# Loading operands ahead at four seams of a split-precision MLP

## The chip, the cores and the metric

The kernel runs on one core of a Trainium2 chip. The metric is the device time of one execution in microseconds (us), as the median of several runs. A core has five engines that run side by side and wait for each other only through semaphores: TensorE (PE in the profile) does matrix products, VectorE (DVE) elementwise work, ScalarE (ACT) copies and activations, GpSimd (POOL) here issues the stores and does some elementwise work, and SyncE (SP) issues the loads. Each engine takes its instructions in the order in which the program put them. The transfers of all queues run on 16 DMA engines.

## The reference

The reference is one layer of an encoder over 2304 tokens (256 and 2048) of width 1024: two mixers, an output projection, and a squared-ReLU MLP with a hidden width of 4096.

```python
def trunk(x, norm1_g, w_in, ...):
    h = rmsnorm(x, norm1_g[l])
    proj = h @ w_in[l]
    ...
    y = jnp.concatenate([ya, yb], axis=-1).astype(x.dtype) @ w_out[l]
    x = x + y
    h = rmsnorm(x, norm2_g[l])
    x = x + jnp.square(jax.nn.relu(h @ w_ff1[l])) @ w_ff2[l]
    return rmsnorm(x, norm_f_g)
```

Everything is fp32. The change touches the last three lines and the way into them.

## The kernel before

**How a product is made.** TensorE works on a rounded 32-bit type (`F32R`). An fp32 operand x is split in two: a high part, which ACT makes by a copy (the instruction `act` on line 83), and a low part, which DVE makes as x minus the high part (`tt`, line 68). `split` does both. `mm3` (lines 176, 179 and 180) adds three products: high by high, high by low, low by high.

**The MLP** is two products of block matrices, each made by a scheme with seven half-sized products in place of eight. In the first product (hidden = h @ w_ff1) the tokens go in three *thirds* (2, then 1, then 0), 2 x 384 tokens each, and a third has 16 *units* of hidden columns; the loop counter n runs from 0 to 47. A unit is seven products p, in the order 1, 6, 2, 7, 5, 3, 4, and each product is 12 matmuls of 128x384. So a unit is 84 matmuls.

- The operands on the token side, one pair of tiles `oh` and `ol` for each p, stay for a whole third. `prep` normalises the tokens (`x1_d`), transposes them and stores their sums as `h2_d` (in the profile h_d); `load_hop` loads them from there in two halves of 128x768 into `xg` tiles and splits each half. There are four `xg` buffers, so SP can have four such loads ahead of the splits.
- The weights come as `w1r` (straight) and `w1t` (sums, stored in `t1_d`), loaded a unit ahead, and each product's weights are split into a tile `w` just before it (six buffers).
- Behind each product, DVE adds it to the others (`u`, `c`), ACT squares it (`hid`), DVE makes the sums (`his`), and POOL stores both in `s2_d` (in the profile s_d).
- `w2_terms` prepares sums of w_ff2 for the second product, once in every second unit from n = 16 on, through `xg` and `gt` tiles.

**The second product** takes its operands two units (one q) at a time: `operands` loads a 128x1280 piece of `s2_d` into a `gt` tile (three buffers) and a 128x1024 piece of weights into an `xg` tile, and splits them into `sh`, `sl`, `th`, `tl`. One q is 30 matmuls of 128x512 over five token blocks j. The residual is loaded from `x1_d` (ten tiles `x1` of 512 KB; x in the profile's names) and added at the end.

**What sets the order.** The program is written as a list of operations; a scheduler decides by a simulated timeline in which order each engine gets them, and tile pools decide which buffer an operation has to wait for. Pools are opened and closed like a stack, so a pool that is opened after another was closed can lie where the other was, and its first writers wait for the last readers of the old tiles. `order(a, b)` and `hold` add an order by hand.

**The seams** that the change touches: (A) the end of the output projection (`out_proj`, `xr` tiles) to the first unit, where lines 1211 to 1217 load and split the seven operands of third 2; (B) third 2 to third 1, and the same from third 1 to third 0, where `load_hop(third - 1, p)` (line 1266) follows the last use of operand p; (C) the first product to the second, where the pools close (line 1270) and the tiles of `operands` are new.

## Time and profile before

| | us |
|---|---|
| median of 3 runs (2749.1 to 2764.31) | 2754.13 |
| the profiled execution | 2757.29 |
| its span, first to last instruction | 2755.5 |
| PE busy | 2602.6 (94%) |
| DVE busy | 1966.1 (71%) |
| ACT busy | 1395.7 (51%) |
| POOL busy | 403.1 (15%) |

Times in the trace are microseconds from the start of the span. The first unit of the MLP begins at 1304.67; seam B lies near 1580, the next one between thirds near 1820, seam C near 2055. A row of a table by stretches gives the stretch and its length, then each engine's busy time and count of instructions, the clock granted to TensorE (1.00 is 2.4 GHz, 0.50 is 1.2 GHz), the busy share of the DMA engines and GB/s. In a row of the timeline an idle time in brackets names what ended it. "pm" and "px_..." are PSUM tiles, "tr", "f2" and "g2" their banks; matmuls overlap, so a mean of one is longer than the distance to the next.

### The profile page before, as it was taken

Reading aid. Unit: us, or ns where it says so; the run is one execution under the profiler, and the core shown is the slowest. Engines: PE = TensorE matmul, PEld = TensorE weight load, DVE = VectorE, ACT = ScalarE, POOL = GpSimd, SP = SyncE. Lnnn points to the kernel's source line nnn. Section 1 sums busy time; section 2 is a strip of 40 time slices with the busy share of each in tenths; the row PEclk is TensorE's granted clock in tenths of the full one; section 3 lists DMA queues with packets and bytes.
Section 4 is the critical chain, followed back from the end, with each engine's and each line's share of the span. In section 5 each row is a group of like instructions: output and inputs, shape, how many; then the busy total and the mean of one; then the engine's idle time right before and its main releaser. Section 6 shows DMA issues by size and latency. Waiting matters only on the chain.

```text
span 2755.5 us, 49048 instructions
## 1 busy us (share of the span) xinstructions
PE 2602.6 (94%) x17846; PEld 2346.1 (85%) x17846; DVE 1966.1 (71%) x5478; ACT 1395.7 (51%) x2608; POOL 403.1 (15%) x666
## 2 busy tenths in 40 slices
PE   6997999879999999999899999999999999999998
PEld 5885699759899987787899899999998888888887
DVE  4783599859899888466888887787765455555564
ACT  5553211248778776234776566666555334344342
POOL 1241223232111111222122011111110000000000
PEclk9999999999999999999899999999999999999999
DMA  9576754488546456799798798898788555775662
GB/s 253 181 240 204 233 175 147 154 235 245 177 149 227 167 193 227 258 336 345 263 321 304 256 343 303 289 348 319 292 309 283 175 172 171 244 239 190 196 224 75
DMA packets 352498, 651.81 MB, mean 237 GB/s; under 512 B 67264, under 2 KB 231744, under 8 KB 346112
## 3 DMA queue, kind: packets, MB, share of 16 engines
q1 hardware_dynamic: 282272, 355.34, 40.2%
q0 software_dynamic: 69984, 293.33, 29.5%
q8 instruction: 141, 2.31, 0.3%
q14 instruction: 101, 0.83, 0.1%
HBM read 428.68 MB, written 219.87 MB: 235 GB/s over the span
## 4 chain that ended last, share of the span: by engine, by line
PE 60%; issue 16%; DVE 8%; DMA 7%; ACT 4%; POOL 4%; SPq 1%; POOLq 0%; DVEq 0%; ACTq 0%
PE pm L176 8%; PE pm L180 8%; PE pm L179 8%; PE px_g L180 3%; PE px_g L176 3%; PE px_g L179 3%; PE px_fl L176 3%; PE px_fl L179 3%; PE px_fl L180 3%; PE px_f L179 3%; PE px_f L180 3%; PE px_f L176 3%; PE px_tr L179 2%; PE px_tr L180 2%; PE px_tr L176 2%
## 5 line engine op out<-in xcount | busy, mean ns | idle before, releaser
L68 DVE TENSOR_TENSOR sl<-gt,sh 128x1280 fp32r<-128x1280 f32 (+1 forms) x112 | 152.1, 1358 | 291.4 <-ACT sh L83 288.9
L83 ACT ACTIVATE sh<-gt 128x1280 fp32r<-128x1280 f32 (+1 forms) x112 | 130.8, 1168 | 393.5 <-PE pm L179 155.8
L176 PE MATMUL px_f<-oh,w 128*128 128x384 f32 x672 | 227.0, 339 | 5.1 <-ACT oh L83 5.1
L180 PE MATMUL pm<-oh,w 128*128 128x384 f32 x672 | 226.5, 337 | 4.3 <-DVE w L68 4.3
L179 PE MATMUL pm<-ol,w 128*128 128x384 f32 x672 | 226.7, 338 | 3.9 <-DVE ol L68 3.9
L176 PE MATMUL pm<-oh,w 128*128 128x384 f32 x672 | 226.3, 338 | 3.7 <-ACT oh L83 3.7
L180 PE MATMUL px_f<-oh,w 128*128 128x384 f32 x672 | 227.5, 339 | 0.8 <-DVE w L68 0.7
L179 PE MATMUL px_f<-ol,w 128*128 128x384 f32 x672 | 227.2, 339 | 0.5 <-DVE ol L68 0.5
L179 PE MATMUL pm<-hl,whi 128*128 128x384 f32 x576 | 201.0, 349 | 7.1 <-DVE hl L80 7.1
L176 PE MATMUL pm<-hh,whi 128*128 128x384 f32 x576 | 198.7, 350 | 7.4 <-ACT sg L83 3.8
L180 PE MATMUL pm<-hh,wlo 128*128 128x384 f32 x576 | 197.9, 345 | 0.0
L83 ACT ACTIVATE sel<-KQ 128x384 f32<-128x384 f32 (+1 forms) x312 | 168.4, 560 | 50.8 <-DVE KQ L68 48.9
L68 DVE TENSOR_TENSOR KQ<-KQ,Fl 128x384 f32<-128x384 f32 x288 | 154.5, 553 | 9.2 <-ACT sel L83 6.9
L83 ACT ACTIVATE w<-w1t 128x512 fp32r<-128x512 f32 x192 | 120.0, 628 | 79.7 <-PE pm L180 43.3
L83 ACT ACTIVATE c<-c 128x384 f32<-128x384 f32 x192 | 99.9, 523 | 100.3 <-DVE c L68 99.5
L176 PE MATMUL pm<-th,sh 128*128 128x512 f32 x384 | 149.7, 391 | 0.0
L68 DVE TENSOR_TENSOR st<-st,pr 128x32 f32<-128x32 f32 (+1 forms) x1016 | 149.6, 202 | 0.0
L179 PE MATMUL pm<-tl,sh 128*128 128x512 f32 x384 | 149.4, 389 | 0.0
L180 PE MATMUL pm<-th,sl 128*128 128x512 f32 x384 | 149.4, 389 | 0.0
L176 PE MATMUL px_g<-th,sh 128*128 128x512 f32 x368 | 143.2, 389 | 0.0
L179 PE MATMUL px_g<-tl,sh 128*128 128x512 f32 x368 | 143.2, 389 | 0.0
L180 PE MATMUL px_g<-th,sl 128*128 128x512 f32 x368 | 143.2, 389 | 0.0
(369 smaller groups left out, 7374.6 us busy)
## 6 DMA issues: line engine op xcount, KB each, us to landing
gt<-s_d SPq DMA_DIRECT2D x112, 384.0 KB
xg<-in_w_ff_dram SPq DMA_DIRECT2D x80, 512.0 KB
s_d<-his POOLq DMA_DIRECT2D x48, 768.0 KB, 7.8
w1t<-t_d SPq DMA_DIRECT2D x32, 1024.0 KB
xg<-t_d SPq DMA_DIRECT2D x64, 512.0 KB
hh<-h_hi POOLq DMA_DIRECT2D x42, 768.0 KB, 7.4
hl<-h_lo POOLq DMA_DIRECT2D x42, 768.0 KB, 6.5
s_d<-hid POOLq DMA_DIRECT2D x48, 576.0 KB, 4.5
```

The source lines that it names most:

```text
L68: ins = V.tensor_tensor(out=o, in0=a, in1=b, op=op)
L83: S.activation(out=o, in_=i, func=f, **kw)
L176: ins = T.matmul(o, ah, bh, start=first, stop=False)
L179: T.matmul(o, ah, bl, start=False, stop=False)
L180: return T.matmul(o, al, bh, start=False, stop=last)
```

## The change

In six parts:

1. The weight pool of the earlier stages, `wp`, is cut from six buffers to four, and two go to a pool `wpb` that is closed earlier (`swb.close()`), so that its room is free when the MLP's pools open.
2. The weights of the first two products of unit 0 are split before the projection's pools close (`first`), into two buffers of a pool that is already open; the six `w` buffers are now 2 + 4. Five of the seven token-side tiles lie in the early pool (four before), and are named by slot and not by p.
3. `load_hop` becomes `raw_hop` (the loads) and `split_hop`. The first half of an operand goes through an `xg` tile, the second half through a `gt` tile.
4. At the two seams between thirds the loads run three operands ahead of the splits.
5. `w2_terms` runs in other units (`W2N` in place of 16, 18, ... 46): none in the first or the last unit of a third (n = 16, 31, 32, 47).
6. The operands of the first two q of the second product are split into old tiles of the first product (the tiles of products 1 and 6, then 2 and 7), before the pools close. The ten residual loads wait for the last matmul of the second q.

The core of the diff:

```diff
-    wp = sww.enter_context(tc.tile_pool(name="wp", bufs=6, reuse_waits="tile"))
+    wp = sww.enter_context(tc.tile_pool(name="wp", bufs=4, reuse_waits="tile"))
+    swb = ExitStack()
+    wpb = swb.enter_context(tc.tile_pool(name="wpb", bufs=2, reuse_waits="tile"))
...
-    def load_hop(third, p):
-        pool = hsa if p in (1, 5, 6, 7) else hsb
-        hop[p] = [pool.tile([P, 4, TB], F32R, name=f"o{x}{p}", tag=f"o{x}{p}") for x in "hl"]
-        for k in range(0, 4, 2):
-            ld = xtile()[:, :2 * TB].rearrange("p (k t) -> p k t", k=2)
+    def slot(pool):
+        return [pool.tile([P, 4, TB], F32R, name=f"o{x}{len(slots)}", tag=f"o{x}{len(slots)}") for x in "hl"]
+
+    def raw_hop(third, p):
+
+        out = []
+        for i, k in enumerate(range(0, 4, 2)):
+            ld = (gtile(2 * TB) if i else xtile()[:, :2 * TB]).rearrange("p (k t) -> p k t", k=2)
             nc.sync.dma_start(out=ld, in_=h2_d[third][:, POS[p], k:k + 2])
-            split(ld, hop[p][0][:, k:k + 2], hop[p][1][:, k:k + 2])
+            out.append(ld)
+        return out
+
+    def split_hop(p, raw, tiles):
+        hop[p] = tiles
+        for i, ld in enumerate(raw):
+            split(ld, tiles[0][:, 2 * i:2 * i + 2], tiles[1][:, 2 * i:2 * i + 2])
...
-    W2S = 16
+
+    W2N = [17, 19, 21, 23, 24, 25, 27, 29, 33, 35, 37, 39, 40, 41, 43, 45]
     ORDER = (1, 6, 2, 7, 5, 3, 4)
+
+    def wtile(x):
+
+        w = (wr1 if x % 6 < 2 else wr).tile([P, 2, 4, P], F32R, name="w", tag="w", bufs=2 if x % 6 < 2 else 4)
+        return w[:, 0], w[:, 1]
...
-    for p in (1, 6, 7, 5):
-        load_hop(2, p)
+    for p in (1, 6, 2, 7, 5):
+        slots.append(slot(hsa))
+        split_hop(p, raw_hop(2, p), slots[-1])
     for b in (1, 0):
         out_proj(b, *out_prep(b, op), op, "f2")
     st6.close()
+    first = [split(w1[0][p], *wtile(x)) for x, p in enumerate(ORDER[:2])]
...
-                wh, wl = split(wt[p], w[:, 0], w[:, 1])
+                wh, wl = first.pop(0) if first else split(wt[p], *wtile(7 * (n - 1) + x))
...
                 if i == NP2 - 1 and third:
-                    load_hop(third - 1, p)
+
+                    if x == 0:
+                        ahead = [raw_hop(third - 1, q) for q in ORDER[:3]]
+                    split_hop(p, ahead.pop(0), hop[p])
+                    if x + 3 < len(ORDER):
+                        ahead.append(raw_hop(third - 1, ORDER[x + 3]))
...
+    early = []
+    for q, (a, b) in enumerate(((1, 6), (2, 7))):
+        (sh, sl), (th, tl) = hop[a], hop[b]
+        early.append(operands(1, q, 0, 5 * P, [t.rearrange("p k t -> p (k t)")[:, :n].rearrange("p (e c) -> p e c", e=2)
+                                               for t, n in ((sh, 1280), (sl, 1280), (th, 1024), (tl, 1024))]))
+    st8.close()
+    st7.close()
...
-        for j in js:
-            for n in range(2):
+        def residuals(after):
+            for j, n in [(j, n) for j in js for n in range(2)]:
                 xt[j, n] = x1p.tile([P, D], F32, name="x1", tag="x1")
-                nc.sync.dma_start(out=xt[j, n], in_=x1_d[tok[j][n]])
+                ld = nc.sync.dma_start(out=xt[j, n], in_=x1_d[tok[j][n]])
+                order(ld, after, mybir.DependencyClass.Sync)
...
             for q in range(late):
-                ops = operands(p, q, j0 * P, j1 * P)
+                ops = early.pop(0) if early else operands(p, q, j0 * P, j1 * P)
                 for j in js:
-                    products(q, j, ops)
+                    mm = products(q, j, ops)
+                if p == 1 and q == 1:
+                    residuals(mm)
```

Up to seam A the engines' orders are the same but for names. What moves at the seams is shown at three places.

DVE at seam A before, from the last additions of the output projection (`xr`) on; `ol1` and `ol6` are low parts of token-side operands of products 1 and 6, `w` low parts of weights, `w1t` sums of the next unit's weights:

```order
L68 TENSOR_TENSOR xr_17291<-xr_17291,px_f2_17307 128x512
L68 TENSOR_TENSOR ol1_17100<-xg_17101,oh1_17099 128x768
L68 TENSOR_TENSOR xr_17322<-xr_17322,px_f2_17324 128x512
L68 TENSOR_TENSOR xr_17322<-xr_17322,px_f2_17338 128x512
L68 TENSOR_TENSOR w1t_17400<-w1r_17399 128x512 x2
L68 TENSOR_TENSOR w_17414<-w1r_17091,w_17414 128x512
L68 TENSOR_TENSOR w_17431<-w1t_17092,w_17431 128x512
L68 TENSOR_TENSOR w1t_17400<-w1r_17399,w1t_17400 128x512
L68 TENSOR_TENSOR w_17448<-w1r_17091,w_17448 128x512
L68 TENSOR_TENSOR w_17468<-w1t_17092,w_17468 128x512
L68 TENSOR_TENSOR w_17485<-w1t_17092,w_17485 128x512
L68 TENSOR_TENSOR w_17506<-w1r_17091,w_17506 128x512
```

and in the changed kernel, where `ol0` to `ol4` belong to products 1, 6, 2, 7, 5:

```order
L68 TENSOR_TENSOR xr_17305<-xr_17305,px_f2_17321 128x512
L68 TENSOR_TENSOR ol0_17104<-xg_17105,oh0_17103 128x768
L68 TENSOR_TENSOR ol1_17114<-xg_17115,oh1_17113 128x768
L68 TENSOR_TENSOR ol2_17124<-xg_17125,oh2_17123 128x768
L68 TENSOR_TENSOR ol3_17134<-xg_17135,oh3_17133 128x768
L68 TENSOR_TENSOR w1t_17410<-w1r_17409 128x512 x2
L68 TENSOR_TENSOR w_17452<-w1r_17095,w_17452 128x512
L68 TENSOR_TENSOR xr_17336<-xr_17336,px_f2_17338 128x512
L68 TENSOR_TENSOR xr_17336<-xr_17336,px_f2_17352 128x512
L68 TENSOR_TENSOR w1t_17410<-w1r_17409,w1t_17410 128x512
L68 TENSOR_TENSOR w_17472<-w1t_17096,w_17472 128x512
L68 TENSOR_TENSOR w_17489<-w1t_17096,w_17489 128x512
```

Four first halves stand ahead of the projection's last two additions, where one stood, and the low parts of the first two products' weights are no longer in this place. Behind the piece shown there stand another `w`, a `w1t`, `ol4` and then the second halves, `ol0` from `gt_17107` first.

SP at seam B before, from the loads of unit 17's weights (`w1r_20486`, `w1t_20487`) on; the operands of products 1 and 6 were loaded earlier, `xg_20342` is the first half of product 2:

```order
L1186 DMA w1r_20486<-in_w_ff1_dram 128x4x256
L1163 DMA xg_20342<-h2_d1_261 128x768
L1163 DMA xg_20346<-h2_d1_261 128x768
L1187 DMA w1t_20487<-t1_d_266 128x2048
L1163 DMA xg_20369<-h2_d1_261 128x768
L1163 DMA xg_20373<-h2_d1_261 128x768
L1163 DMA xg_20400<-h2_d1_261 128x768
L1163 DMA xg_20404<-h2_d1_261 128x768
L1185 DMA w1r_20635<-in_w_ff1_dram 128x4x128
```

and now, where `xg_20328` is the first half of product 5 and `gt_20305` the second half of product 7:

```order
L1198 DMA w1r_20464<-in_w_ff1_dram 128x4x256
L1169 DMA xg_20328<-h2_d1_264 128x768
L1169 DMA gt_20305<-h2_d1_264 128x768
L1199 DMA w1t_20465<-t1_d_269 128x2048
L1169 DMA xg_20356<-h2_d1_264 128x768
L1169 DMA gt_20330<-h2_d1_264 128x768
L1169 DMA xg_20381<-h2_d1_264 128x768
L1169 DMA gt_20358<-h2_d1_264 128x768
L1242 DMA xg_20613<-in_w_ff2_dram 128x1024
L1242 DMA xg_20614<-in_w_ff2_dram 128x1024
L1169 DMA gt_20383<-h2_d1_264 128x768
```

Seven of the fourteen half loads stand further up, where four did, and the last of them (`gt_20383`, the second half of product 4) stands behind two loads of `w2_terms`.

SP at the start of the second product before; `gt_25630` belongs to the third q, `gt_25673` to the fourth, `xg_25719` to the fifth, and `x1_d` is the residual:

```order
L1296 DMA gt_25630<-s2_d2_265 128x2x384
L1296 DMA gt_25630<-s2_d1_264 128x2x256
L189 DMA gf_25517<-in_norm_f_g_dram 128x1024
L1319 DMA x1_25519<-x1_d12_280 128x1024
L1319 DMA x1_25521<-x1_d15_283 128x1024
...
L1319 DMA x1_25537<-x1_d10_278 128x1024
L1296 DMA gt_25673<-s2_d2_265 128x2x384
L1296 DMA gt_25673<-s2_d1_264 128x2x256
L1298 DMA xg_25719<-in_w_ff2_dram 128x2x512
```

and now, where `gt_25641` belongs to the fourth q, `gt_25684` to the fifth, `xg_25730` and `gt_25727` to the sixth, `gt_25770` to the seventh:

```order
L1305 DMA gt_25641<-s2_d1_267 128x2x256
L1307 DMA xg_25687<-in_w_ff2_dram 128x2x512
L1305 DMA gt_25684<-s2_d2_268 128x2x384
L1305 DMA gt_25684<-s2_d1_267 128x2x256
L1307 DMA xg_25730<-in_w_ff2_dram 128x2x512
L191 DMA gf_25511<-in_norm_f_g_dram 128x1024
L1352 DMA x1_25578<-x1_d12_283 128x1024
...
L1352 DMA x1_25596<-x1_d10_281 128x1024
L1305 DMA gt_25727<-s2_d2_268 128x2x384
L1305 DMA gt_25727<-s2_d1_267 128x2x256
L1305 DMA gt_25770<-s2_d2_268 128x2x384
```

The ten residual loads stand behind the pieces of five q where they stood behind those of three, and the first of them now waits on PE.

## Rows read from the trace of the kernel before

**Rows 1.** The page's first part: busy time of each engine.
```profile
PE 2602.6 (94%) x17846; PEld 2346.1 (85%) x17846; DVE 1966.1 (71%) x5478; ACT 1395.7 (51%) x2608; POOL 403.1 (15%) x666
```

**Rows 2.** Busy time by stretches: busy us (count) per engine, clock, DMA.
```profile
1305.00:1330.00 25.00, 15.63 (x52) 13.46 (x51) 20.24 (x30) 12.03 (x18) 1.59 (x3) 0.66 0.85 309
1500.00:1550.00 50.00, 47.77 (x270) 46.35 (x269) 37.20 (x71) 22.86 (x46) 5.76 (x10) 1.00 0.66 228
1580.00:1600.00 20.00, 14.82 (x57) 13.84 (x58) 18.09 (x31) 13.22 (x25) 1.59 (x3) 0.74 0.93 316
1600.00:1800.00 200.00, 200.00 (x1156) 200.00 (x1155) 158.84 (x283) 121.10 (x223) 23.38 (x44) 1.00 0.86 309
1800.00:1850.00 50.00, 49.20 (x279) 47.91 (x278) 44.65 (x75) 36.00 (x64) 3.72 (x7) 1.00 0.94 342
2055.00:2070.00 15.00, 12.14 (x43) 9.40 (x44) 9.00 (x10) 8.00 (x9) 0.53 (x1) 0.77 1.00 369
2100.00:2740.00 640.00, 640.00 (x2825) 529.92 (x2825) 341.72 (x507) 235.51 (x243) 7.44 (x14) 1.00 0.58 190
```

**Rows 3.** Waits of PE at seam A: waited for, us, times, longest.
```profile
PE px_f L176 <- ACT oh L83: 3.0, 2, 2.3
PE pm L180 <- DVE w L68: 2.2, 1, 2.2
PE pm L179 <- DVE ol L68: 2.1, 1, 2.1
```

**Rows 4.** Timeline of SP's queue at seam A.
```profile
1291.89 0.32 SPq L1163 DMA_DIRECT2D xg<-h_d  x1
...
1301.31 2.21 SPq L1163 DMA_DIRECT2D xg<-h_d  x4
...
1312.47 17.39 SPq L1163 DMA_DIRECT2D xg<-h_d  x9
```

**Rows 5.** Timeline of PE at seam A: the first matmul of unit 0.
```profile
1304.67 0.33 PE L176 MATMUL pm<-oh,w 128*128 128x384 f32 x1
```

**Rows 6.** Timeline of DVE at seam A: third addition before the projection's end.
```profile
1299.43 0.69 DVE L68 TENSOR_TENSOR xr<-xr,px_f 128x512 f32<-128x512 f32 x1 [2.03 <-PE px_f L180]
```

**Rows 7.** Groups of DVE instructions, shapes apart, 1550 to 1600.
```profile
L68 DVE TENSOR_TENSOR ol<-xg,oh 128x768 fp32r<-128x768 f32 x12 | 11.3, 949 | 0.3 <-ACT oh L83 0.3
L68 DVE TENSOR_TENSOR w<-w1t,w 128x512 fp32r<-128x512 f32 x14 | 9.6, 684 | 2.3 <-ACT w L83 2.3
...
L1115 DVE TENSOR_TENSOR his<-hid 128x384 f32<-128x384 f32 x8 | 4.1, 552 | 3.8 <-DMA s_d<-his 3.8
```

**Rows 8.** Groups of ACT instructions, shapes apart, 1550 to 1600.
```profile
L83 ACT ACTIVATE oh<-xg 128x768 fp32r<-128x768 f32 x12 | 9.8, 835 | 4.8 <-DMA xg<-h_d 4.8
```

**Rows 9.** Waits of PE at seam B, 1570 to 1600.
```profile
PE pm L176 <- ACT oh L83: 1.9, 1, 1.9
```

**Rows 10.** Timeline of SP's queue at seam B: the loads of product 2.
```profile
1570.65 1.67 SPq L1163 DMA_DIRECT2D xg<-h_d  x2
```

**Rows 11.** Waits of PE at seam C, 2040 to 2100.
```profile
PE px_tr L176 <- ACT th L83: 3.9, 1, 3.9
```

**Rows 12.** Timeline of ACT at seam C: the third and the fourth q's `sh`.
```profile
2066.82 1.27 ACT L83 ACTIVATE sh<-gt 128x1280 fp32r<-128x1280 f32 x1 [6.96 <-issue]
...
2072.70 1.28 ACT L83 ACTIVATE sh<-gt 128x1280 fp32r<-128x1280 f32 x1 [2.70 <-DMA gt<-s_d]
```

**Rows 13.** Timeline of SP's queue at seam C.
```profile
2045.87 12.65 SPq L1319 DMA_DIRECT2D x<-x_d  x10
2059.20 0.95 SPq L1296 DMA_DIRECT2D gt<-s_d  x2
```

**Rows 14.** DMA totals, 2058 to 2080.
```profile
DMA packets 3982, 8.66 MB, mean 394 GB/s; under 512 B 293, under 2 KB 1977, under 8 KB 3981
```

**Rows 15.** Groups of DVE instructions, shapes apart, 2050 to 2100.
```profile
L68 DVE TENSOR_TENSOR sl<-gt,sh 128x1280 fp32r<-128x1280 f32 x11 | 16.4, 1491 | 13.6 <-ACT sh L83 13.0 <-PE pm L179 0.5
L68 DVE TENSOR_TENSOR tl<-xg,th 128x1024 fp32r<-128x1024 f32 x11 | 13.3, 1218 | 0.0
```

More of the change, by code (lines that the diff above doesn't have):

```diff
@@ L513, in hybrid_trunk_kernel @@
     stage1_norm(1)
-    wv = [row_unit(w_in, 256 * i, 1536, wx if i < 2 else None) for i in range(4)]
+    wv = [row_unit(w_in, 256 * i, 1536, wx if i < 2 else wpb) for i in range(4)]
     stage1_proj(0)
@@ L647, in hybrid_trunk_kernel @@
         stage2_v(b, mark if b == VL[0] else None)
-    wqq = [col_unit(w_in, h * P, wx if h < 2 else None) for h in range(NH)]
+    wqq = [col_unit(w_in, h * P, wx if h < 2 else wpb) for h in range(NH)]
     for b in range(NB - NL):
@@ L702, in weights @@
     def weights(h):
-        wq[h] = [col_unit(w_in, n * 512 + h * P) for n in (1, 2)]
+        wq[h] = [col_unit(w_in, n * 512 + h * P, wpb if h == 2 else None) for n in (1, 2)]
     def gelu(b):
@@ L1023, in hybrid_trunk_kernel @@
     oq, XQ = st5.enter_context(tc.tile_pool(name="oq", bufs=3, reuse_waits="tile")), 3
-    wo5 = [[row_unit(w_out, 512 + 256 * i, dh * 512) for i in range(2)] for dh in range(2)]
+    wo5 = [[row_unit(w_out, 512 + 256 * i, dh * 512, wpb if dh else None) for i in range(2)] for dh in range(2)]
     wo = [[row_unit(w_out, 256 * i, 0) for i in range(2)]]
@@ L1095, in hybrid_trunk_kernel @@
     hpool.close()
+    swb.close()
     st6 = ExitStack()
@@ L1148, in prep @@
             GP.dma_start(out=h2_d[third][:, :, k, j * P:(j + 1) * P], in_=ch[:, 1:])
-    hop = {}
+    hop, slots = {}, []
     def gtile(n):
@@ L1213, in hybrid_trunk_kernel @@
     psum_open(st8, f2=3)
-    for p in (2, 3, 4):
-        load_hop(2, p)
+    for p in (3, 4):
+        slots.append(slot(hsb))
+        split_hop(p, raw_hop(2, p), slots[-1])
     def w2_terms(i):
@@ L1234, in hybrid_trunk_kernel @@
                 prep(1 - (n - 1) // NCB, (n - 1) % NCB)
-            if n >= W2S and (n - W2S) % 2 == 0 and n < W2S + 2 * NP2:
+            if n in W2N:
                 hold[0] = last
-                w2_terms((n - W2S) // 2)
+                w2_terms(W2N.index(n))
                 hold[0] = None
@@ L1247, in hybrid_trunk_kernel @@
                 o = ptile("mm" if (7 * n + x) % 2 else "f2", TB)
-                w = wr.tile([P, 2, 4, P], F32R, name="w", tag="w")
-                wh, wl = split(wt[p], w[:, 0], w[:, 1])
+                wh, wl = first.pop(0) if first else split(wt[p], *wtile(7 * (n - 1) + x))
                 hh, hl = hop[p]
@@ L1269, in hybrid_trunk_kernel, with operands @@
             GP.dma_start(out=s2_d[third][:, i, 3:7], in_=fs)
[L1270 to L1289 removed]
+    w2v = w_ff2.rearrange("(q m p) c -> p q m c", m=2, p=P)
+    def operands(p, q, c0, c1, tiles=None):
         qs = slice(2 * q, 2 * q + 2)
@@ L1298, in operands, with bank9 @@
         nc.sync.dma_start(out=tr, in_=w2v[:, qs, p != 1, (512 if p == 3 else 0):(1024 if p == 3 else 512)] if p < 4 else t2_d[:, qs, {5: 0, 6: 1, 7: 2, 4: 3}[p]])
-        sh, sl = split(sr, op9.tile([P, 2, 640], F32R, name="sh", tag="sh")[:, :, :w], op9.tile([P, 2, 640], F32R, name="sl", tag="sl")[:, :, :w])
-        th, tl = split(tr, op9.tile([P, 2, 512], F32R, name="th", tag="th"), op9.tile([P, 2, 512], F32R, name="tl", tag="tl"))
-        return sh, sl, th, tl
+        if tiles is None:
+            tiles = [op9.tile([P, 2, n], F32R, name=x, tag=x)[:, :, :m] for x, n, m in (("sh", 640, w), ("sl", 640, w), ("th", 512, 512), ("tl", 512, 512))]
+        return [*split(sr, *tiles[:2]), *split(tr, *tiles[2:])]
+    early = []
[5 more added lines that the diff above has]
+    st7.close()
+    st9 = ExitStack()
+    x1p = st9.enter_context(tc.tile_pool(name="x1p", bufs=10, reuse_waits="tile"))
+    t9 = st9.enter_context(tc.tile_pool(name="t9", bufs=1, reuse_waits="tile"))
+    op9 = st9.enter_context(tc.tile_pool(name="op9", bufs=6, side="right", reuse_waits="tile"))
+    psum_open(st9, g2=3)
+    gf = bcast_load(t9, "gf", norm_f_g)
+    nbank = [0]
+    def bank9():
+        nbank[0] += 1
+        return ptile(("tr", "tr", "mm", "mm", "mm", "g2", "g2", "g2")[nbank[0] % 8 - 1], 512)
     def final(t, xt, queue):
```

16 lines of the change are left out of this document (2 added, 14 removed).

## The prediction

> **What bounds the kernel now.** I read the engines' totals first: PE is busy 94% of the span, no other engine above 71% [rows 1]. So time can only be won where PE stands or runs at the lower clock, and the table by stretches says where that is [rows 2]. At full speed PE does 1156 matmuls of 128x384 in 200 us (0.173 us each) and 2825 of 128x512 in 640 us (0.2265 each), with no idle time in either stretch. At the three seams the same rows show three losses:
>
> - Seam A: 25 us hold 52 matmuls, worth 52 x 0.173 = 9.0 us; 16.0 are lost. PE stood 25 - 15.6 = 9.4 of them; the other 6.6 are the clock, granted at 0.66 on average, so partly at its lower level of 1.2 GHz.
> - Seam B: 20 us hold 57, worth 9.9; 10.1 lost, 5.2 of them standing and 4.9 clock (0.74).
> - Seam C: 15 us hold 43 matmuls, nearly all 128x512, worth 9.7; 5.3 lost, and about 1 more just ahead of the stretch, since the one stall is 3.9 [rows 11] and only 2.9 of it lie inside: 6.3, of which 2.4 clock.
>
> The seam from third 1 to third 0 loses only 0.8. Another 2.2 stand at 1500 to 1550 in waits that the change does not touch. What the change can win is thus 16.0 + 10.1 + 6.3 + 0.8 = 33 us, 1.2% of the run.
>
> Next come the waits and queues at each seam. At A PE waits in turn for ACT's `oh`, DVE's `ol` and a low part of weights [rows 3]; SP issues one half load at 1291.89, four more at 1301.31 and the other nine only from 1312.47 [rows 4], since the four `xg` buffers come free with DVE's splits. At B it waits for `oh` and `ol` [rows 9]; the loads of product 2 go out at 1570.65 [rows 10], late because DVE was held 3.8 us by stores of `his` [rows 7]. At C it waits for ACT's `th`, whose new tile could not be written before the old pools were done.
>
> **The change part by part.**
>
> *Weight pool in two parts.* The same loads and splits in the same order up to seam A; 0. If a buffer came late there, it would show as a wait of DVE or ACT under 1 us; I give it 0 to +1.
>
> *Seam A.* Unit 0 begins at 1304.67 [rows 5], bound to the end of the projection, and that stays. Now the first halves of five products are there early: 5 x 6 matmuls x 0.173 = 5.2 us of work. What is late next is DVE. In its new order the first `ol` follows the addition that began at 1299.43 [rows 6], so from 1300.1: four `ol` of 0.95 [rows 7] to 1303.9; two `w1t` and a `w` at 0.68 to 1306.0; two `xr` at 0.69 to 1307.4; a `w1t`, three `w`, a `w1t` to 1310.8; `ol4` to 1311.8; the second half of `ol0` to 1312.7. PE has done products 1, 2, 6 and 7's first halves at 1304.67 + 4.2 = 1308.8 and wants `ol4` then: 3.0 us of stall. After it, PE needs 1.04 us a half and DVE 0.95 and some small operations; about equal, no more than another 0.5. The transfers say the same: the first second half goes out behind four first halves and a 512 KB load, 4 x 0.39 + 0.52 + its own 0.39 = 2.1 MB (the first of them issued once a split of 1301.0 has freed a buffer), which at the 309 GB/s of the stretch [rows 2] take 6.8 us from 1304, to 1310.8; `oh` adds 0.84 [rows 8]. With a clock loss in the old proportion (6.6 to 9.4) 3.5 us of stall cost 6.0. So A goes from 16.0 to 6.0: **-10**, with bounds -14 (a stall of 1) and -4 (two more waits of 3 us each, for products 7 and 4, whose second halves stand behind loads of weights and of the residual tokens).
>
> *Seam B.* Seven half loads of fourteen stand ready in place of four, and the loads for products 5 and 7 go out where those for product 2 did, for a use 4 us later (two products of 2.08). That covers both stalls of about 1.8. But DVE is busy 18.1 of 20 us there; it has 14 splits of 0.95 to fit, and the hold by `his` is not touched. `w2_terms` no longer falls into the first unit, which frees four operations of 0.68, 2.7 us. The nearest row for what is left is the next seam, with the same 14 splits and a loss of 0.8; one full stall and its clock (1.9 + 1.8) is the other end. I take 3.6 left: **-6.5**, bounds -9.5 and 0. For the seam from third 1 to third 0 I take 0 (-0.8 to +3).
>
> *Seam C.* The first two q are split within the last unit, in tiles that PE left one to four products before. DVE gets 2 x (1.49 + 1.22) = 5.4 us more there [rows 15], beside about 10 of its own in 14.5, so it ends a little late, but its late work is the last unit's `his`, for which PE does not wait. PE goes on at once: the stall of 3.9 and its clock go. A new wait comes at the third q: its `tl` lies where q 1 is read, so DVE can write it only when that q is done, 2 x 30 x 0.2265 = 13.6 us after the first product's end T. It takes 1.22; PE has five matmuls of `th` by `sh` first, 1.1. Cost 0.1 to 0.8 with clock. The third `sh` had to wait until 2066.82, 12.9 us after T, for a store [rows 12]; that store now runs without the ten residual loads beside it, so it should land before 13.6. I take **-5.5**, bounds -6.3 and -1.
>
> *The residual loads.* They leave SP between T and T + 13.6 and go out after it; behind them in SP's queue stand the pieces of the sixth and the seventh q. The last wait there: 10 x 0.52 + 0.66 = 5.9 MB at the 394 GB/s seen with such loads [rows 14] are 15.0 us, so the sixth q's piece lands at T + 28.6, or with 2 us from issue to landing T + 30.6; `sh` ends at T + 31.9. PE wants it at T + 5 x 6.8 = T + 34.0. So 0, with 2 us to spare; at the 309 GB/s of seam A it would come 2 us too late, 3.4 with clock.
>
> The Trainium skill speaks against this step: "DMA: Bandwidth & Descriptors", section "Rules for kernel authors", says to issue a transfer early and wait for it late, and its section "Specifications" gives a core some 358 GB/s from memory. An estimate from that page is 16.5 us for the 5.9 MB, which leaves 0.6 us to spare; with any other transfer beside it the sixth q stalls, by some 3.4 as above, and the sum below is -18.6. The trace differs on the rate: 394 GB/s over 22 us [rows 14]. It also shows what the early loads cost: the fourth q's piece went out behind them at 2059.20 [rows 13] and its `sh` began 13.5 us later [rows 12].
>
> *`w2_terms` in other units.* Same number, 2.7 us of DVE each; a unit has about 10 of 14.5 busy without one, so three in a row still fit. 0.
>
> Sum: -10 - 6.5 - 5.5 = -22. The profiled execution took 2757.3 (span 2755.5), so 2735.3 for one like it; it lies 3.2 above the median of the runs shown, 2754.1, from which I predict **2732** (0.8%).
>
> **The rivals.**
>
> 1. *The stalls only move.* A and B are held by DVE (18 to 20 busy of 20 to 25) and by the DMA engines (0.85 and 0.93 busy), and loading earlier adds no room to either. For: those rows, and PE waits for both ACT and DVE in turn. Against: the third seam, with the same work, loses 0.8, and at A the nine loads wait for buffers until 1312.47 while DMA is not full. A keeps 12, B keeps 7, C keeps the q 5 stall of 3.4: -4 - 3 - 3 = -10, **2744**.
> 2. *Nearly all goes.* Splits ahead of the additions cover A to 2 us, B ends like the next seam, C at 0: -14 - 9.3 - 6.3 = -30, **2724**.
> 3. *One queue for everything* (slower). At both seams between thirds SP holds weight loads behind half loads that wait for a `gt` buffer, that is for a split on a full DVE. If `w1t` goes out so late that it lands after the unit that reads it has begun (it is loaded a unit, 14.5 us, ahead), the unit waits for it and every later split moves back: B keeps its 10.1 and adds a wait like the 2.2 for a low part of weights with clock, 4; the next seam becomes such a seam too, +14; C -6. Sum +12, **2766**. For: the order at B has `w1t_20465` behind `gt_20305`. Against: before, it stood behind two such loads as well.
> 4. *It does not do what it says.* The scheduler could have put the early splits late; the orders shown have them early, so only a wait that no order shows could do it: 2754.
>
> **How the numbers follow.** Forecast 0.56 (2725 to 2741 by its own bounds), rival 1 0.25, rival 2 0.12, rival 3 0.05, rival 4 0.02. 0.5% is 13.8 us, about what a measurement of this kernel can tell from no change (its three runs span 15). Faster than 2740.4: most of the forecast (0.5), rival 2 and a little of rival 1: 0.65. Within: the rest of both, and rival 4: 0.30. Slower than 2767.9: half of rival 3 and what I cannot name, 0.05. The range takes in rival 2 with some spread of the runs below it, and rival 1 with its upper bound: 2720 to 2752.
>
> **What would show it.** Right: in 1305 to 1330 PE holds 95 or more matmuls, in place of 52, with one wait for DVE's `ol` or ACT's `oh` near 3 us; between the thirds no wait over 1 us and the clock at 1.00 for the most part; at C no wait for `th`, a short one for `tl` 13.6 us later, and none at the sixth q. Wrong: a wait for `sh` behind DMA some 34 us after T; waits at A that add up to 8 again, for `ol` (DVE's order) or `oh` (transfers); DVE full and PE waiting for `w` at either seam between thirds; or waits before 1160, where nothing should differ.

## The result and the profile after

The changed kernel takes 2719.8 us (median; 2715.7 to 2722.5), the kernel before beside it 2751.6: a ratio of 0.987, 95% interval 0.9853 to 0.9887. By the two medians 31.8 us are saved, by the ratio 36 (31 to 40). The forecast was 2732, the range 2720 to 2752. It lies 0.2 us below the range, beyond rival 2 ("nearly all goes", 2724), and the gain is half as large again as forecast.

The profiled execution of the changed kernel took 2722.5 us, span 2720.7. First the stretches that answer to [rows 2], and one that was not looked at before, 1350 to 1500. The table by stretches of the changed kernel:

```profile
1305.00:1330.00 25.00, 21.20 (x105) 17.83 (x106) 23.50 (x57) 18.11 (x30) 1.60 (x3) 1.00 1.02 380
1350.00:1500.00 150.00, 150.00 (x896) 149.58 (x895) 135.10 (x387) 108.77 (x222) 36.66 (x51) 1.00 0.92 327
1500.00:1550.00 50.00, 48.79 (x278) 47.74 (x277) 39.75 (x74) 28.05 (x56) 5.32 (x10) 1.00 0.71 250
1570.00:1600.00 30.00, 29.81 (x170) 29.16 (x170) 28.07 (x51) 20.22 (x40) 4.25 (x8) 1.00 1.00 362
1800.00:1850.00 50.00, 50.00 (x290) 50.00 (x290) 42.15 (x76) 33.15 (x65) 5.83 (x11) 1.00 0.87 323
2025.00:2055.00 30.00, 29.74 (x131) 24.29 (x131) 11.54 (x12) 8.62 (x10) 1.06 (x2) 1.00 0.73 272
```

PE does 105 matmuls in 1305 to 1330 where it did 52, at the full clock. Both seams between thirds and seam C are all but gone. The same table of the kernel before for the stretch that the prediction did not look at:

```profile
1350.00:1500.00 150.00, 145.43 (x869) 143.30 (x868) 131.77 (x397) 108.62 (x221) 36.46 (x50) 1.00 0.89 315
```

There PE stood 4.6 us, all of it in the early units, where the transposes of `prep` (`px_tr`) waited for ACT. Waits of PE in the kernel before, 1350 to 1500:

```profile
PE px_tr L1144 <- ACT gt L83: 2.5, 2, 2.2
PE px_tr L1144 <- ACT xg L83: 2.1, 3, 1.3
```

In this execution of the changed kernel it does not stand there at all.

To see where the time went, the MLP is cut by three events that the order has in common: the first matmul of unit 0, the fourteenth store of `hid` (before: 1554.72, after: 1537.41), and the last matmul of the first product (2053.53 and 2024.82). Microseconds in each stretch:

```
                unit 0 begins   to 14th hid   to product's end   to the end
before               1304.7         250.1           498.8           702.0
changed              1303.3         234.2           487.4           695.9
difference             -1.4         -15.9           -11.4            -6.1
```

The sum is -34.8, 3 us more than the medians give, against a forecast of -22 (-10, -6.5, -5.5). Seam A lies in the second column, B and the next seam in the third, C in the fourth. The second column can be cut once more by the sixth store of `hid`: -13.2 up to it, -2.7 behind it. Of the -13.2, the waits at transposes before 1429 are 3.9 (0.4, 2.2 and 1.3), so seam A is about -9.3, and the early units -6.6. Counted in the prediction's own way seam A comes out the same: 105 matmuls are worth 18.2 us, so 6.8 of the 25 are lost where 16.0 were, -9.2.

### The profile page after: what moved, and what is told of

Read it like the earlier page. It is cut to its first block, busy times and chain, and to the rows that moved or that the text cites. A ratio compares the mean times of both kernels' runs of the same rounds, so it can differ in the third digit from the quotient of the medians.

```text
span 2720.7 us, 49044 instructions
## 1 busy us (share of the span) xinstructions
PE 2592.2 (95%) x17846; PEld 2337.8 (86%) x17846; DVE 1967.1 (72%) x5478; ACT 1396.9 (51%) x2608; POOL 402.5 (15%) x666
## 3 DMA queue, kind: packets, MB, share of 16 engines
q0 software_dynamic: 69984, 293.33, 29.8%
## 4 chain that ended last, share of the span: by engine, by line
PE 64%; issue 14%; DMA 8%; DVE 7%; POOL 3%; ACT 3%; SPq 1%; POOLq 0%; DVEq 0%; ACTq 0%
PE pm L178 9%; PE pm L182 9%; PE pm L181 9%; PE px_f L182 4%; PE px_f L181 4%; PE px_f L178 4%; PE px_g L182 3%; PE px_g L178 3%; PE px_g L181 3%; DMA w1r<-in_w_ff_dram 3%; PE px_fl L178 2%; PE px_fl L181 2%; PE px_fl L182 2%; PE px_tr L181 2%; PE px_tr L182 2%
## 5 line engine op out<-in xcount | busy, mean ns | idle before, releaser
L68 DVE TENSOR_TENSOR sl<-gt,sh 128x1024 fp32r<-128x1024 f32 (+1 forms) x110 | 149.2, 1356 | 281.4 <-ACT sh L83 281.4
L83 ACT ACTIVATE sh<-gt 128x1024 fp32r<-128x1024 f32 (+1 forms) x110 | 128.2, 1166 | 382.0 <-PE pm L181 147.8
L68 DVE TENSOR_TENSOR KQ<-KQ,Fl 128x384 f32<-128x384 f32 x288 | 154.2, 552 | 10.1 <-ACT sel L83 7.8
L68 DVE TENSOR_TENSOR w<-w1t,w 128x512 fp32r<-128x512 f32 x192 | 131.1, 684 | 18.1 <-ACT w L83 15.4
```

The costliest lines, as they stand in the source:

```text
L68: ins = V.tensor_tensor(out=o, in0=a, in1=b, op=op)
L83: S.activation(out=o, in_=i, func=f, **kw)
```

## The experiments

All are read by the same three stretches, from one profile each, beside the medians and the ratios to the kernel before.

```
                begin  to 14th hid  to prod. end  to end    median   ratio (95%)
before          1305      250.1        498.8      702.0     2751.6
changed         1303      234.2        487.4      695.9     2719.8   0.9870 (0.9853-0.9887)
again           1315      232.9        487.6      695.9     2720.9   0.9882 (0.9859-0.9905)
a_xg            1309      250.6        490.6      695.9     2736.3   0.9950 (0.9931-0.9969)
late_x1         1303      240.7        489.4      695.9     2730.4   0.9932 (0.9912-0.9951)
no_ahead        1307      235.0        487.6      695.9     2722.2   0.9883 (0.9857-0.9909)
w2_even         1306      236.3        487.5      695.9     2726.8   0.9895 (0.9871-0.9919)
no_first        1306      230.7        489.1      695.9     2722.0   0.9887 (0.9857-0.9917)
no_early        1305      235.3        487.4      708.1     2737.1   0.9942 (0.9928-0.9957)
res_first       1300      239.9        488.6      697.2     2728.1   0.9904 (0.9888-0.9921)
gt_only         1301      230.1        488.8      703.3     2729.3   0.9904 (0.9882-0.9926)
gt_A            1311      241.5        494.7      702.2     2737.9   0.9945 (0.9922-0.9968)
gt_B            1300      249.0        492.9      702.4     2746.7   0.9971 (0.9958-0.9985)
c_only          1310      250.6        495.2      695.9     2751.3   0.9988 (0.9972-1.0003)
gt_c            1300      233.6        489.4      695.9     2719.8   0.9877 (0.9855-0.9899)
```

One profile of each has a spread that bounds what a column can tell. The first column (the work ahead of the MLP, which the experiments leave alone but for its end) varies by 15 us from execution to execution. Seven profiles have the changed kernel's order of instructions all through the second column (changed, again, no_ahead, w2_even, no_first, no_early, res_first), and it runs from 230.7 to 239.9 in them. The third runs from 487.4 to 489.1 in the six of these whose order is the same there too, up to the last unit; but before and c_only, likewise with one order up to there, have 498.8 and 495.2. The last column is steady to 0.1 where its order is that of the changed kernel.

The 3.6 us between before and c_only lie at seam B. The stretch of c_only that answers to 1580 to 1600 in [rows 2]:

```profile
1586.00:1606.00 20.00, 15.04 (x74) 13.96 (x73) 19.43 (x33) 15.65 (x29) 1.60 (x3) 0.91 0.93 322
```

PE stands as long as before (5.0 us and 5.2), but the clock is 0.91 in place of 0.74, and 74 matmuls are done in place of 57. With the old order seam B thus costs 7.2 us in one execution and 10.1 in another, and what the change takes from the third column is 7.8 to 11.4 us.

**Taking one part out of the changed kernel**

*a_xg: both halves at seam A through the `xg` buffers.*

```diff
-        split_hop(p, raw_hop(2, p), slots[-1])
+        split_hop(p, raw_hop(2, p, False), slots[-1])   # False: no gt tile; at both places
...
```

> The changed kernel, but at seam A both halves of each token-side operand go through the four xg buffers again (the gt buffers are used only at the seams between thirds). SP's order then has the x1 loads of prep behind all fourteen half loads again, as before the change. Theory: the waits of PE for transposes at 1397 to 1478 (4.6 us before, none after) and for a low part of weights at 1517 to 1552 (2.8 before, 1.0 after) went because prep's loads were freed from that place. So they come back, 4 to 7 us, beside 3 to 9 us lost at seam A itself; 2727 to 2735, ratio to before about 0.990 to 0.994. Rival: those waits went because seam A itself got shorter or because the scheduler shuffled the early units by chance. Then the transposes' waits stay away (under 1 us) and only seam A loses; 2723 to 2728.

2736.3 us, just past the theory's 2727 to 2735. Waits of PE in a_xg at seam A, 1305 to 1340, then in the early units, 1340 to 1510 (waited for: us, times, longest):

```profile
PE pm L178 <- ACT oh L83: 6.3, 3, 3.7
PE px_f L178 <- ACT oh L83: 4.4, 4, 1.8
...
PE px_tr L1147 <- ACT gt L83: 11.0, 5, 3.4
```

and SP's queue, where all four of prep's first loads come behind the half loads:

```profile
1336.09 3.35 SPq L1136 DMA_DIRECT2D xg<-x_d  x4
```

as they did in the kernel before:

```profile
1329.53 0.32 SPq L1163 DMA_DIRECT2D xg<-h_d  x1
1331.23 5.06 SPq L1133 DMA_DIRECT2D xg<-x_d  x4
```

So the second set of buffers is what opened both seam A and the early units. Two things are open. The transposes wait 11.0 us here and 4.6 in the kernel before, with these loads behind the half loads in both. And the waits for a low part of weights near 1517 to 1552, which the theory had coming back, did not. Seam B does not need the second set at A: the third column stays at 490.6, but it uses `gt` there itself.

*no_ahead: no lead at the seams between thirds.*

```diff
-                    if x == 0:
-                        ahead = [raw_hop(third - 1, q) for q in ORDER[:3]]
-                    split_hop(p, ahead.pop(0), hop[p])
-                    if x + 3 < len(ORDER):
-                        ahead.append(raw_hop(third - 1, ORDER[x + 3]))
+                    split_hop(p, raw_hop(third - 1, p), hop[p])
```

> The changed kernel, but at the seams between thirds each operand's loads are issued at its split and not three operands ahead (halves still through xg and gt). Theory of the prediction: the lead is what removes the stalls of seam B (10.1 us with the clock before, nothing after), so B loses 4 to 10 again, 2724 to 2730. Rival: two sets of buffers are enough, since seven halves can be under way in place of four, or moving w2_terms out of the first unit is; then B stays under 1 us and the time is 2718 to 2722, not told from the changed kernel.

487.6 us in the third column, as in the changed kernel, and PE works 29.8 of 30 us at the seam. The stretch 1575 to 1605 of no_ahead:

```profile
1575.00:1605.00 30.00, 29.82 (x170) 29.05 (x170) 27.21 (x50) 19.97 (x39) 3.72 (x7) 1.00 0.98 361
```

But this run is no test of the lead. In its trace every engine's instructions of the MLP stand, by their names, in the order of the changed kernel, SP's loads at the seam included: the scheduler sends the loads ahead by itself as far as there are buffers for them. So the lines that ask for a lead of three change nothing here, and what the order would be worth without its lead was not tried.

*w2_even: w2_terms in every second unit again.*

```diff
-    W2N = [17, 19, 21, 23, 24, 25, 27, 29, 33, 35, 37, 39, 40, 41, 43, 45]
+    W2N = list(range(16, 48, 2))
```

> The changed kernel with w2_terms in units 16, 18, ... 46 as before. Theory: with two sets of buffers DVE's 2.7 us in the first unit of a third are covered and the seams between thirds lose under 1 us together: within 1.5 us of the changed kernel. Rival: DVE is the bound at the seams (28.1 us busy of 30 at 1570 to 1600 in the changed kernel), so 2.7 us more in the first unit come out as 1 to 3 us of waits at each of the two seams, with or without the clock: 2722 to 2730.

The third column is 487.5, so the theory holds at the seams. The median is 7 us above the changed kernel's, where the theory had 1.5. The profile is 4.5 longer, all of it in the first two columns, where the order is the same, and the intervals of the two ratios overlap: it is taken for the spread of the executions. At the seam:

```profile
1575.00:1605.00 30.00, 29.82 (x171) 29.38 (x170) 29.93 (x56) 20.07 (x39) 4.80 (x9) 1.00 1.01 369
```

DVE is busy 29.9 of 30 us, and PE still stands 0.2. A full DVE is not a late DVE: what it does in time and what it does behind time look alike in its busy share.

*no_first: the first weights of unit 0 with the others.*

```diff
-    first = [split(w1[0][p], *wtile(x)) for x, p in enumerate(ORDER[:2])]
+    first = []
```

> The changed kernel without the early split of the first two products' weights in unit 0 (they are split with the others, in the same six buffers). Theory: DVE has two w more between the first ol and the projection's last additions or behind them, 2 x 0.68; PE waits that much longer for a low part at its first or third product, 1 to 3 us at seam A: 2721 to 2724. Rival: DVE has the same sum of work up to ol4 and PE's waits only change places, under 1 us: 2718 to 2721.

2722.0, the second column 230.7: no loss. But here too the trace has every engine's order, by the names, as in the changed kernel: the scheduler splits these weights as early without the added line. So neither the theory nor the rival was put to the test; the line changes nothing.

*no_early: new tiles for the first operands of the second product.*

```diff
-    for q, (a, b) in enumerate(((1, 6), (2, 7))):
+    for q, (a, b) in ():
```

> The changed kernel, but all operands of the second product go into new tiles after the pools close; the residual loads still wait for the last matmul of the second q. Theory: the stall for th at seam C comes back with its lower clock, 3.9 + 2.4 = 6.3 us less the 0.3 that the changed kernel waits there: about 2726, ratio 0.989. Rival: the residual loads ahead of the product were part of the stall (they hold the store of his and the fourth q), so with them out of the way the stall is 1 to 3 us and the clock stays: 2721 to 2723.

Both were wrong on the size: the last column grows by 12.2 us. The wait of PE at seam C, and ACT's first `sh`:

```profile
PE px_tr L178 <- ACT th L83: 10.2, 1, 10.2
```
```profile
2035.44 1.27 ACT L83 ACTIVATE sh<-gt 128x1280 fp32r<-128x1280 f32 x1 [6.18 <-DMA s_d<-his]
```

ACT waits for the last store of `his` before it can write the first new tile, so in the changed kernel's layout that tile seems to lie where `his` was. In the kernel before it waited for no store, and PE stood 3.9 us [rows 11]. ACT's first `sh` there:

```profile
2055.55 1.25 ACT L83 ACTIVATE sh<-gt 128x1280 fp32r<-128x1280 f32 x1
```

So in the changed kernel the early operands of part 6 are worth 12.2 us, and in the kernel before the whole part 6.1 (c_only, below). That it is the moved pools that would have made seam C dearer is likely, but was not tried alone.

*res_first: the residual loads ahead of the first q.*

```diff
-                order(ld, after, mybir.DependencyClass.Sync)
+                if after is not None:
+                    order(ld, after, mybir.DependencyClass.Sync)
...
+            if p == 1:
+                residuals(None)
...
-                if p == 1 and q == 1:
-                    residuals(mm)
```

> The changed kernel, but the ten residual loads are issued before the first q again and wait for nothing on PE. Theory: they go out at about T, the end of the first product, beside the last store of his, which then lands 12 to 13 us after T in place of 9; the third q's sh waits for it and ends at about T + 14.2, so PE waits 0.5 to 2 us at T + 13.6, with no lower clock: 2720 to 2723. Rival: the place of these loads is worth nothing (within 0.3 us of the changed kernel in the waits of PE), or earlier is better because the sixth q's piece lands earlier: 2717 to 2720.

As the theory said, in the last column: 697.2 in place of 695.9, for a wait of PE at the third q, whose `sh` waits for the last store of `his`. That store was issued at 2033.32, 8.1 us before; in the changed kernel it is 5.0.

```profile
PE px_tr L178 <- ACT th L83: 1.0, 1, 1.0
```
```profile
2041.45 1.27 ACT L83 ACTIVATE sh<-gt 128x1280 fp32r<-128x1280 f32 x1 [10.56 <-DMA s_d<-his]
```

The rest of the 8 us between the medians is ahead of seam C, where the two kernels' orders are equal. In this profile a transpose of `prep` waits 2.9 us, which none did in the changed kernel's; why is open.

**One part alone, in the kernel before**

*gt_only: the second half of an operand through a `gt` tile.*

```diff
-            ld = xtile()[:, :2 * TB].rearrange("p (k t) -> p k t", k=2)
+            ld = (gtile(2 * TB) if k else xtile()[:, :2 * TB]).rearrange("p (k t) -> p k t", k=2)
```

> The kernel before with one edit: the second half of each token-side operand goes through a gt tile, the first through xg as before. No lead of three, the old pools, the old w2_terms, the old seam C. Theory: two sets of buffers are what opened seam B and the early units; B's 10.1 us go to under 2, the waits for transposes and w in third 2 shrink from 7 to under 4, and seam A gains 4 to 9 of its 16 (product 2 is still loaded after the projection's pools close). Sum -15 to -24: ratio 0.991 to 0.9945. Rival: the room made by the pools and the slots is needed for any of it, since product 2 is late at A, and without the lead B loads late: -3 to -8, ratio 0.997 to 0.999.

The theory holds, a little past its better end: 0.9904 (0.9882 to 0.9926) for 0.991 to 0.9945, and the first two stretches of the MLP are those of the changed kernel (230.1 and 488.8). Waits of PE in gt_only, 1340 to 1600, all of them:

```profile
PE pm L176 <- DVE c L68: 0.3, 1, 0.3
```

and at seam C, 2000 to 2060, which this edit leaves:

```profile
PE px_tr L176 <- ACT th L83: 3.9, 1, 3.9
PE px_tr L179 <- DVE tl L68: 0.7, 1, 0.7
```

*gt_A and gt_B: the same edit at seam A only, and at the seams between thirds only.*

```diff
+            ld = (gtile(2 * TB) if k and third == 2 else xtile()[:, :2 * TB])...   # gt_A; gt_B: third < 2
```

> The kernel before with second halves through gt tiles at seam A only (third 2); the seams between thirds as before. Theory: at A the gt tiles let SP put prep's x1 loads ahead of the last half loads, so A loses under 8 us with the clock in place of 16 and the transposes wait under 1 us in place of 3 to 5; seam B keeps its 5 us of stalls and its clock, and the waits for a low part of weights at 1517 to 1552 stay near 2.8. About 2740, ratio 0.994 to 0.996. Rival: the waits in the early units come from the scheduler's chance or from the run, not from this edit: transposes still wait 2 to 5 us, ratio over 0.996.

> The kernel before with second halves through gt tiles only at the two seams between thirds; seam A as before. Theory: B's stalls go from 5 to under 0.5 us and its clock stays at 1.00, and the waits for w at 1517 to 1552 go too if they come from the half loads for third 1 that stand ahead of weight loads there; A keeps 9 to 11 us and its clock, the transposes 2 to 11. About 2741, ratio 0.994 to 0.997. Rival: B needs A's part as well, since it is a lag from earlier units that reaches it: B keeps 3 us or more.

gt_A gains 8.6 us in its column, and its ratio is the theory's; a transpose still waits 2.7, for the theory's under 1. Its third column, 494.7, is that of c_only (495.2), where seam B is as before, so the edit at A gains nothing there that shows. In gt_B the waits for `oh` and `ol` are gone from seam B, but others stand in their place. Waits of PE in gt_B, 1545 to 1600:

```profile
PE px_f L180 <- DVE w L68: 2.1, 2, 1.6
PE pm L180 <- DVE w L68: 1.3, 2, 0.9
PE pm L176 <- DVE c L68: 0.9, 1, 0.9
PE pm L176 <- ACT p L83: 0.4, 1, 0.4
```

So the rival on gt_B holds: B keeps waits of 4.7 us, now mostly for weights, where it has under 1 with the edit at both places. By the third column it keeps 5.5 of the 7.8 to 11.4. Which of the earlier units' delays reaches B in this way was not tried.

*c_only: part 6 alone.*

> The kernel before with the sixth part alone: the operands of the first two q of the second product in old tiles of the first product, the residual loads behind the last matmul of the second q. Theory: this part is worth what seam C lost, 6.0 us in the profiles (3.9 of stall and 2.4 of clock, 0.3 left), and nothing else moves: ratio to before 0.9978, about 2747 beside a before of 2753. Rival: taking the split of the first product's last unit onto DVE costs as much as it saves, or the residual loads starve the sixth q: within 2 us of before.

(The edit is that part of the diff, in the kernel before.) The last column says 695.9: -6.1, what the theory said, to 0.1. The ratio, 0.9988 (0.9972 to 1.0003), cannot tell that from nothing; its interval holds both.

*gt_c: the two together; again: the changed kernel once more.*

> The kernel before with two parts: second halves through gt tiles at all seams, and the operands of the first two q of the second product in old tiles with the residual loads behind them. No lead, no new pools, no early weights, the old w2_terms. Theory: these two are the change; the rest is worth nothing that the waits of PE show: the waits add up to 9 to 13 us from 1150 on as in the changed kernel (10.3), the ratio to before is 0.987 to 0.989 and within 2 us of the changed kernel. Rival: pools, early weights and lead are worth some us at A and B: 3 to 8 us slower than the changed kernel run beside it.

> The changed kernel once more, beside the kernel before and the kernel with the two parts. Theory: 0.9870 again (0.986 to 0.988), the same stalls at seam A (3 to 4 us) and the clock lost after them or not, as it comes; transposes under 3 us. Rival: the first profile was lucky: waits from 1150 on add up to over 14 us, and the ratio is over 0.988.

2719.8 and 2720.9, ratios 0.9877 and 0.9882: with these two parts the kernel is as fast as with all six, within about 0.2%. The second profile of the changed kernel has the same stretches as the first but for the work ahead of the MLP. The theory on gt_c holds. That on again holds in the waits of PE (9.9 us from 1150 on, none at a transpose of `prep`), and its ratio is 0.0002 past the bound.

**What moved in the early units**

*late_x1: prep's loads behind all half loads, nothing else.*

```diff
             xt = xtile()
-            nc.sync.dma_start(out=xt, in_=x1_d[(2 * third + n) * NCB + j])
+            ld = nc.sync.dma_start(out=xt, in_=x1_d[(2 * third + n) * NCB + j])
+            if hop:
+                order(ld, hop["last"])
...
-            nc.sync.dma_start(out=ld, in_=h2_d[third][:, POS[p], k:k + 2])
+            hop["last"] = nc.sync.dma_start(out=ld, in_=h2_d[third][:, POS[p], k:k + 2])
```

> The changed kernel, but SP issues prep's loads of the residual tokens (x1) behind all fourteen half loads of seam A, as before the change; the halves still go through both sets of buffers. Theory: the two sets of buffers matter in the early units because they let these loads go ahead. Then the stretch from unit 0 to the fourteenth store of hid, 233 to 240 us in runs of the changed kernel and 250 before, goes to 242 or more, with waits for transposes of 3 to 11 us, and the time to 2727 or more (ratio 0.990 or more). Rival: the early units gain because seam A itself is short and DVE and ACT carry less of a lag out of it; then the stretch stays at 230 to 238 with transposes under 3 us, seam A is even 1 to 2 us shorter since DVE has no small operations of prep between its splits, and the time is 2714 to 2722.

The changed kernel sends prep's first loads between the half loads, from 1304.43 on; late_x1 sends all four behind them. SP's queue in the changed kernel, then in late_x1:

```profile
1304.43 0.32 SPq L1136 DMA_DIRECT2D xg<-x_d  x1
1304.92 1.27 SPq L1169 DMA_DIRECT2D gt<-h_d  x3
...
1316.67 1.26 SPq L1136 DMA_DIRECT2D xg<-x_d  x2
```
```profile
1324.19 3.21 SPq L1136 DMA_DIRECT2D xg<-x_d  x4
```

Waits of PE in late_x1, 1340 to 1500; in the two profiles of the changed kernel no transpose waited there:

```profile
PE px_tr L1149 <- ACT xg L83: 3.2, 1, 3.2
PE px_tr L1149 <- ACT gt L83: 2.2, 1, 2.2
PE pm L178 <- DVE c L68: 1.7, 1, 1.7
```

The median is 2730.4, the ratio 0.9932 (0.9912 to 0.9951), as the theory said, and clear of the changed kernel's; the column is 240.7, between the two and by itself too close to the 239.9 of res_first to tell. About 10 us by the medians thus hang on where four loads stand in one queue. That is more than the 7.1 of these waits; the lower clock behind them (0.83 in 1455 to 1475) and the spread are the likely rest.

## Why the prediction was wrong

By its own steps:

- *Weight pool, early weights (0).* Right: gt_c has neither and is as fast, and no_first has the same order without the early weights.
- *Seam A (-10).* Right in sum, about -9.3, and partly by luck. DVE's times came out almost to the number; what PE lost is made up otherwise. Stalls of PE in the changed kernel, then DVE at the place that the prediction worked through:

```profile
1306.26 0.44 PE L182 MATMUL pm<-oh,w 128*128 128x384 f32 x1 [1.43 <-DVE w L68]
1306.54 0.33 PE L178 MATMUL pm<-oh,w 128*128 128x384 f32 x1
...
1311.33 0.44 PE L181 MATMUL pm<-ol,w 128*128 128x384 f32 x1 [1.54 <-DVE rs_x L77]
```
```profile
1310.33 0.95 DVE L68 TENSOR_TENSOR ol<-xg,oh 128x768 fp32r<-128x768 f32 x1
...
1311.83 0.96 DVE L68 TENSOR_TENSOR ol<-gt,oh 128x768 fp32r<-128x768 f32 x1
```

  `ol4` ended at 1311.3 (forecast 1311.8), the second half of `ol0` at 1312.8 (1312.7). The two stalls make 3.0, as forecast, but only the second is the one worked through (for `ol4`; the row names the small operation behind it). The first is for a low part of weights. The clock stayed at its upper level, so the 2.5 us counted for it were not paid; something else of that size was. Of the 6.8 us lost in 1305 to 1330, 3.8 are PE standing, and the other 3.0 go at full clock, at a dozen short waits: after each the first matmuls follow each other more slowly, as at 1306.54, 0.28 us after the one before it in place of 0.17. Two sums of the working are wrong and decided nothing: the loads it calls 2.1 MB are 2.5 by their own terms, which would have brought the first second half to 1312.0 (its `oh` began at 1310.8), and the bound of -4 counts two waits of 3 us without the clock that it counts elsewhere.
- *Seam B (-6.5).* Mis-sized: with the next seam -11.4 by this pair of profiles, -7.8 beside c_only. The step was "DVE is busy 18.1 of 20 us there ... I take 3.6 left", the far end of its own two rows (0.8 and 3.7). Under 1 us is left (1570 to 1600 holds 170 matmuls, worth 29.4 us of the 30), with DVE as full as before (28.1 of 30), and also with `w2_terms` put back (w2_even, 29.9 of 30). The row nearest in kind, the next seam's 0.8 [rows 2], would have given -9.3. The reason for the gain, seven half loads ready in place of four, stands. What makes them seven is the second set of buffers; the lines that ask for a lead add nothing (no_ahead). The 10.1 that it started from is one execution's: 7.2 in c_only.
- *The early units (0).* The step that failed. "What the change can win is thus ... 33 us" counted the seams alone, and "another 2.2 stand at 1500 to 1550 in waits that the change does not touch" was wrong: they went to 1.2 with it, and 4.6 us of waits for transposes at 1397 to 1478 were not in the sum at all. They were in the trace. The prediction even names prep's loads ("of the residual tokens") as standing ahead of the last half loads, but only as a risk for seam A; it did not ask what their moving up would free. a_xg and late_x1 show it. Their size, -6.6, is that of one pair of profiles: the second column of the same order spreads by 9, and a transpose waits up to 2.9 in it. What freed the waits at 1500 to 1550 is open, as they stay away in a_xg too.
- *Seam C (-5.5).* Right: -6.1, 0.3 left as a wait for `tl` 15 us after the product's end (forecast 13.6).

```profile
PE px_tr L181 <- DVE tl L68: 0.3, 1, 0.3
```

- *The residual loads (0).* Right. In the changed kernel they go out 13.8 us after the product's end at 2025.0; ACT's third q, then the sixth:

```profile
2034.40 1.27 ACT L83 ACTIVATE sh<-gt 128x1280 fp32r<-128x1280 f32 x1 [7.46 <-DMA s_d<-his]
...
2055.99 1.27 ACT L83 ACTIVATE sh<-gt 128x1280 fp32r<-128x1280 f32 x1 [13.03 <-DMA gt<-s_d]
```
```profile
2038.83 5.15 SPq L1352 DMA_DIRECT2D x<-x_d  x10
2045.19 4.17 SPq L1305 DMA_DIRECT2D gt<-s_d  x4
```

  The sixth q's `sh` ended at 2057.3, T + 32.3 (forecast T + 31.9), for a use at T + 34. res_first issues these loads early and is 1.3 us slower in that column, since the store of `his` that the third q waits for lets ACT go on only 8.1 us after its issue beside them, and 5.0 without. The Trainium skill ("DMA: Bandwidth & Descriptors", section "Rules for kernel authors") says to issue a transfer early and wait for it late; this trace does not bear that out here, where a store that is waited for sooner runs beside the early loads.
- *w2_terms elsewhere (0).* Right (w2_even).

Of the 12.8 us between forecast and this pair of profiles, 6.6 are the early units, 4.9 seam B (1.3 beside c_only), 0.6 seam C, 1.4 the work ahead of the MLP, which varies by 15 and is no effect; A gave 0.7 less. So the early units are the step that failed, and seam B the term that was mis-sized.

Rival 1 (the stalls only move) fell: the only stall that took another's place was the two of 1.5 at A. Rival 2 came nearest, with 2724, but not by its terms: it had A at 2 us, where 6.8 are lost, and nothing for the early units. Rival 3 fell: no wait for `w` grew.

## What to carry to other kernels

Where loads wait for buffers that are freed by the splits of the loads before them, look for another set of buffers that is idle at that time; here one line that sends every second load through it was worth 0.96% of the kernel by itself (0.7 to 1.2), and with one other part it did all that six did. When a load moves up in a queue, list what moves up behind it, and look for its waits in the whole trace and not only at the seam. An engine's busy share near one says little about whether others wait for it: take the nearest place where the same work ran, and believe its loss. And where a scheduler sets the order, compare the orders of two runs before you read the second as a test of a part: here two runs without a part had the order of the run with it.

## What the runs showed of the hardware

- Two stalls at seam A left the clock at 1.00 in both profiles of the changed kernel (1.4 and 1.5 us in the first, 1.7 and 1.5 in the second). With the same order there, in no_early, stalls of 0.8 and 1.5 took it to its lower level for a while. The stretch 1300 to 1325 of the changed kernel, then of no_early:

```profile
1300.00:1325.00 25.00, 21.34 (x103) 17.16 (x101) 22.51 (x48) 17.58 (x28) 1.60 (x3) 1.00 1.02 387
```
```profile
1300.00:1325.00 25.00, 22.48 (x106) 19.38 (x104) 22.20 (x47) 17.04 (x28) 2.16 (x4) 0.93 1.03 402
```

  So what a stall of this size costs in clock can't be read from one execution. Seam B in the old order says the same: PE stood 5.2 and 5.0 us, at a mean clock of 0.74 and 0.91.
- A short wait of PE costs more than the time it stands, at the full clock too: at seam A of the changed kernel 3.8 us of standing went with 6.8 us lost.
- The last store of `his` (768 KB) let ACT go on 5.0 us after its issue (2029.36 to 2034.40) with no other loads beside it, and 8.8 us after it (2058.06 to 2066.82 [rows 12]) beside the ten residual loads; in res_first, beside them as well, 8.1 us.
